# Other row pitches, offsets and product orders for the split activations of a two-layer decoder

## The chip, the cores and the metric

The kernel runs on one core of a Trainium2 chip. The metric is the device time of one execution in microseconds. Three runs of the kernel before took 2369.81 to 2370.03 us, median 2370.01 us. A core has a matrix engine (PE, with its weight loads shown as PEld), a vector engine (DVE), an activation engine (ACT), a general engine (POOL) and a queue engine (SP), which run on their own and wait for one another by semaphores. SBUF is the on-chip memory with 128 partitions; PE reads both operands from it and writes to PSUM.

## The reference

A decoder trunk of two layers over 272 tokens (16 learned meta tokens, then 256) of width 2048, 16 heads of 128. Layer 0 uses forgetting attention, layer 1 stick-breaking attention over a K/V computed once; each is followed by a squared-ReLU MLP of hidden width 8192.

```python
def squared_relu_mlp(h, w_up, w_down):
    u = h @ w_up
    return jnp.square(jax.nn.relu(u)) @ w_down

for layer in range(DEPTH):                                   # 2
    a = rms_norm(h, norm_attn[layer])
    if layer < N_A_LAYERS:                                   # layer 0
        q, k, v, f_logit = jnp.split(a @ fox_w_in[i], [D_MODEL, 2 * D_MODEL, 3 * D_MODEL], axis=-1)
        logf = jax.nn.log_sigmoid(f_logit + fox_b_f[i])
        o = forgetting_attention(q, k, v, cumsum(logf))      # softmax(q k / sqrt(128) + F_q - F_k), causal
        h = h + o @ fox_w_o[i]
    else:                                                    # layer 1
        shared_k, shared_v = jnp.split(rms_norm(h, kv_norm) @ w_kv, 2, axis=-1)
        o = stick_breaking_attention(a @ sb_w_q[i], shared_k, shared_v)
        h = h + o @ sb_w_o[i]
    h = h + squared_relu_mlp(rms_norm(h, norm_mlp[layer]), w_up[layer], w_down[layer])
return rms_norm(h, final_norm)[:, N_META:]
```

All of it is float32, and the result has to keep float32 accuracy.

## The kernel before

The residual stream lies feature major in SBUF: `hT` [128, 16 chunks, 272 tokens]. PE has a fast format, float32r, that keeps fewer bits than float32. Each float32 operand of a large product is therefore split into a high part (the value rounded to float32r) and a low part (the rest), and a product becomes three: high weights x high activations, high weights x low activations, low weights x high activations.

`new_split` (line 99) gives the split activations of one stage as a tile [128, 16 chunks, 2, 272] float32r out of a pool of two buffers: for each chunk 272 high values, then 272 low ones. A chunk row is 2 x 272 x 4 = 2,176 bytes, 8.5 times 256. In the built program the two buffers begin at bytes 92,800 and 127,616 of each partition, both 128 past a multiple of 256. Stages of layer 1 that need only the 256 real tokens skip the first 16 columns (64 bytes) of each part.

`gemm_group` (line 146) makes four output chunks of 128 features, over all of K. It goes over four quarters of K: a DMA on SP brings 512 x 512 weights (`raw`, 1 MiB), ACT rounds them to `whi` (line 174), DVE subtracts to get `wlo` (line 175), in two halves of two chunks each. For each (chunk, output) place it issues the three products of lines 195 to 197 into one of four PSUM accumulators:

```python
nc.tensor.matmul(accs[m][:, :n], wh, hi[:, k, t0:], start=first, stop=False)     # L195
nc.tensor.matmul(accs[m][:, :n], wh, lo[:, k, t0:], start=False, stop=False)     # L196
nc.tensor.matmul(accs[m][:, :n], wl, hi[:, k, t0:], start=False, stop=last)      # L197
```

With `pairs` (stages o1 and down projections of layer 1) the first two become one product of 2 x 256 columns (line 193); the evacuation then adds two halves. A stage of four groups is 4 x 64 places, so 768 products, or 512 with `pairs`.

The stages in order, with the names of their activations: q, k, v of layer 0 (`x_a`, 12 groups, attention between them), output projection (`x_o`), four blocks of up (`x_m`) and down projection (`x_u`); for layer 1 the queries (`x_a`, 256 columns), k and v (`x_kv`, 8 groups, attention between them), output projection (`x_o`, pairs), four blocks of up (`x_m`) and down (`x_u`, pairs). Layer 0 and k, v use 272 columns, the others 256.

The order on each engine is not that of the source: a scheduler that simulates the time places the instructions. Where `wlo` comes late, it puts off the products of line 197 and takes hi and lo products of further outputs first. `split_chunk` (line 103), `put_split` (line 290) and the evacuation in `mlp` (line 420) write the split activations; `Norm.finish` (line 127) makes the inverse root of the mean squares.

Of the kernel before, what the change touches and what calls it, by code (L numbers as in the profile page):

```python
# [24 lines left out]
N_FF = 4             # blocks of D columns in the hidden width  # L25
# rows of the gains
# [4 lines left out]
def yoco_kernel(ctx: ExitStack, tc: tile.TileContext, hT_in, gains, b_f, w_f, w_qkv0, w_o0, w_up, w_dn,  # L31
# [5 lines left out]
    wspl = ctx.enter_context(tc.tile_pool(name="wspl", bufs=3))  # L37
    xs = ctx.enter_context(tc.tile_pool(name="xs", bufs=2))
# [21 lines left out]
    # ntri[k', k] = -1 where k' >= k  # L60
# [6 lines left out]
    # causal mask of the first layer, on negated scores [query, key]: keys of the queries 16..143,  # L67
    # then of the queries 144..271
# [6 lines left out]
    # the same for the meta tokens of four heads, [head and query, (head, key)] with room for 32 keys  # L75
# [6 lines left out]
    # strict mask of the second layer [key, query]: keys 0..127 x queries 16..271, then  # L82
    # keys 128..255 x queries 128..271
# [6 lines left out]
    # tokens 256..271 of four heads, [head and key, (head, query)]  # L90
# [12 lines left out]
    def split_chunk(sp, gi, c, t0):  # L103
        """gain * residual chunk, as two float32r parts that add up to it"""
        hi, lo, _ = sp
        g = g_sb[:, gi, c:c + 1]
        nc.scalar.activation(hi[:, c, t0:], hT[:, c, t0:], AF.Copy, scale=g)
        nc.vector.scalar_tensor_tensor(out=lo[:, c, t0:], in0=hT[:, c, t0:], scalar=g,
                                       in1=hi[:, c, t0:].bitcast(F32), op0=ALU.mult, op1=ALU.subtract)

    class Norm:
        """sum of squares of the residual stream, chunk by chunk, and its inverse root"""
# [14 lines left out]
        def finish(self):  # L127
# [3 lines left out]
            a = tmp.tile([P, T], F32, tag="rs_a", bufs=1, name=f"rs_a_{self.label}")  # L131
            y = tmp.tile([P, T], F32, tag="rs_y", bufs=1, name=f"rs_y_{self.label}")
            t = tmp.tile([P, T], F32, tag="rs_t", bufs=1, name=f"rs_t_{self.label}")
# [12 lines left out]
    def gemm_group(wblk, sp, t0, evac, before={}, after={}, load_x=None, pairs=False):  # L146
# [4 lines left out]
        hi, lo, both = sp  # L151
# [4 lines left out]
        for kb in range(4):  # L156
# [28 lines left out]
            for kc, m in order:  # L185
                whi, wlo = parts[kc // 2]
                k = 4 * kb + kc
                wh = whi[:, kc % 2, m * P:(m + 1) * P]
                wl = wlo[:, kc % 2, m * P:(m + 1) * P]
                first = kb == 0 and kc == 0  # L190
                last = kb == 3 and kc == 3
                if pairs:
                    nc.tensor.matmul(accs[m], wh, both[:, k, :, t0:], start=first, stop=False)  # L193
                else:
                    nc.tensor.matmul(accs[m][:, :n], wh, hi[:, k, t0:], start=first, stop=False)  # L195
                    nc.tensor.matmul(accs[m][:, :n], wh, lo[:, k, t0:], start=False, stop=False)  # L196
                nc.tensor.matmul(accs[m][:, :n], wl, hi[:, k, t0:], start=False, stop=last)  # L197
                if last:
                    evac(m, [accs[m][:, :n]] + ([accs[m][:, n:]] if pairs else []))
# [5 lines left out]
    def total(acc, to):  # L205
        """the sum of the parts of a product, in SBUF if there are two"""
# [6 lines left out]
    # ================= layer 0: forgetting attention =================  # L213
    norm = Norm("a0", 0)
    xa = new_split("a0")
    box = {}

    def load_x(chunks):
        c0, n = chunks[0], len(chunks)
        nc.sync.dma_start(hT[:, c0:c0 + n, :], hT_in[:, c0:c0 + n, :])  # L220
        for c in chunks:
            split_chunk(xa, G_A0, c, 0)
# [11 lines left out]
    def forget_gates(rstd):  # L234
        """log sigmoid, running sum over the tokens"""
# [8 lines left out]
        for k in range(NC):  # L244
            nc.tensor.matmul(pf[:NC, :T], wf_hi[:, k, :], xa[0][:, k, :], start=k == 0, stop=False)
            nc.tensor.matmul(pf[:NC, :T], wf_hi[:, k, :], xa[1][:, k, :], start=False, stop=False)
            nc.tensor.matmul(pf[:NC, :T], wf_lo[:, k, :], xa[0][:, k, :], start=False, stop=k == NC - 1)
# [11 lines left out]
        # tokens 16..143 and 144..271 on the partitions  # L259
# [4 lines left out]
        # by way of DRAM for the copies to all partitions  # L264
# [4 lines left out]
    def token_major(vT, pr, t0, label):  # L269
        """tokens t0 .. t0+127 and t0+128 .. t0+255 of two heads"""  # L270
# [8 lines left out]
    def packed(src, label):  # L279
        """[128, 4, n] in consecutive columns"""  # L280
# [5 lines left out]
    def put_split(sp, h, nh, t, n, src):  # L286
        nc.scalar.activation(sp[0][:, h:h + nh, t:t + n], src, AF.Copy)
# [356 lines left out]
```

## Time and profile before

| | |
|---|---|
| median of three runs | 2370.01 us |
| span of the profiled execution | 2368.6 us |
| PE busy | 2351.3 us (99%), 17,758 matmuls |
| weight loads | 2281.5 us (96%), 17,758 |
| DVE busy | 1320.9 us (56%) |
| ACT busy | 1037.9 us (44%) |
| POOL busy | 35.1 us (1%) |
| DMA | 412 MB, 174 GB/s |

The profile tells busy time of each engine, its groups of instructions by line, the chain of work that ended last, and a timeline with the start of each instruction. Matmuls are pipelined: each lasts longer in the record than the distance to the next one's start, so the rate of PE is read from start to start. Lines (L195) are those of the kernel. An entry `acc<-x_u,whi 128*128 128x272` is a product of 128 x 128 high weights with 272 columns of `x_u` into an accumulator.

### The profile page before, as it was taken

Reading aid. Unit: us, or ns where it says so; the run is one execution under the profiler, and the core shown is the slowest. Engines: PE = TensorE matmul, PEld = TensorE weight load, DVE = VectorE, ACT = ScalarE, POOL = GpSimd, SP = SyncE. Lnnn points to the kernel's source line nnn. Section 1 sums busy time; section 2 is a strip of 40 time slices with the busy share of each in tenths; the row PEclk is TensorE's granted clock in tenths of the full one; section 3 lists DMA queues with packets and bytes.
Section 4 is the critical chain, followed back from the end, with each engine's and each line's share of the span. In section 5 each row is a group of like instructions: output and inputs, shape, how many; then the busy total and the mean of one; then the engine's idle time right before and its main releaser. Section 6 shows DMA issues by size and latency. Waiting matters only on the chain.

```text
span 2368.6 us, 41443 instructions
## 1 busy us (share of the span) xinstructions
PE 2351.3 (99%) x17758; PEld 2281.5 (96%) x17758; DVE 1320.9 (56%) x1837; ACT 1037.9 (44%) x1393; POOL 35.1 (1%) x61
## 2 busy tenths in 40 slices
PE   8999999999999999999999999999999999999998
PEld 8999999999999999999999999989989989989997
DVE  7565555655455455445565555566555555555555
ACT  5433344543344344344444444445443443543444
POOL 0000000000000000000000000000000000000000
PEclk9999999999999999999999999999999999999999
DMA  6444444554545555455555444455555555555553
GB/s 231 143 167 170 152 161 161 171 185 162 185 170 178 178 178 178 165 178 174 178 177 188 153 144 143 144 176 180 194 179 194 194 180 195 179 180 196 185 188 125
DMA packets 60872, 412.08 MB, mean 174 GB/s; under 512 B 7040, under 2 KB 9744, under 8 KB 11920
## 3 DMA queue, kind: packets, MB, share of 16 engines
q1 hardware_dynamic: 59632, 407.05, 50.3%
q8 instruction: 139, 2.28, 0.4%
q10 hardware_dynamic: 1056, 2.38, 0.3%
q14 instruction: 45, 0.37, 0.0%
HBM read 407.29 MB, written 2.11 MB: 173 GB/s over the span
## 4 chain that ended last, share of the span: by engine, by line
PE 99%; DVE 0%; DMA 0%; ACT 0%; issue 0%; SPq 0%; DVEq 0%
PE acc L197 32%; PE acc L196 25%; PE acc L195 25%; PE acc L193 12%; PE ps L332 0%; PE pza L507 0%; PE pv L274 0%; PE po L393 0%; PE po L394 0%; PE po L546 0%; DVE ob L590 0%; PE po L547 0%; PE pzb L508 0%; DMA raw<-w_qkv 0%; PE po L395 0%; PE po L548 0%
## 5 line engine op out<-in xcount | busy, mean ns | idle before, releaser
L175 DVE TENSOR_TENSOR wlo<-raw,whi 128x1024 fp32r<-128x1024 f32 (+1 forms) x770 | 934.6, 1221 | 808.7 <-ACT whi L174 806.1
L174 ACT ACTIVATE whi<-raw 128x1024 fp32r<-128x1024 f32 (+1 forms) x770 | 807.2, 1056 | 1144.1 <-PE acc L196 874.4
L196 PE MATMUL acc<-x_m,whi 128*128 128x272 f32 (+1 forms) x2048 | 577.5, 285 | 0.0
L195 PE MATMUL acc<-x_m,whi 128*128 128x272 f32 (+1 forms) x2048 | 574.6, 284 | 0.0
L197 PE MATMUL acc<-x_m,wlo 128*128 128x272 f32 (+1 forms) x2048 | 559.4, 285 | 0.0
L197 PE MATMUL acc<-x_u,wlo 128*128 128x272 f32 (+1 forms) x2048 | 537.1, 285 | 0.0
L197 PEld LDWEIGHTS acc<-x_u,wlo 128*128 128x128 f32 x2048 | 381.1, 188 | 13.5
L196 PEld LDWEIGHTS acc<-x_m,whi 128*128 128x128 f32 x2048 | 386.7, 189 | 0.0
L195 PEld LDWEIGHTS acc<-x_m,whi 128*128 128x128 f32 x2048 | 386.3, 189 | 0.3
L197 PEld LDWEIGHTS acc<-x_m,wlo 128*128 128x128 f32 x2048 | 376.2, 188 | 0.0
L193 PE MATMUL acc<-x_u,whi 128*128 128x512 f32 x1024 | 342.8, 395 | 0.0
L195 PE MATMUL acc<-x_a,whi 128*128 128x272 f32 (+1 forms) x1024 | 293.4, 290 | 6.3 <-ACT whi L174 6.3
L196 PE MATMUL acc<-x_a,whi 128*128 128x272 f32 (+1 forms) x1024 | 294.1, 291 | 0.0
L195 PE MATMUL acc<-x_u,whi 128*128 128x272 f32 x1024 | 292.6, 288 | 0.0
L196 PE MATMUL acc<-x_u,whi 128*128 128x272 f32 x1024 | 292.1, 288 | 0.0
L197 PE MATMUL acc<-x_a,wlo 128*128 128x272 f32 (+1 forms) x1024 | 284.1, 289 | 0.0
L193 PEld LDWEIGHTS acc<-x_u,whi 128*128 128x128 f32 x1024 | 186.2, 188 | 30.9
L195 PEld LDWEIGHTS acc<-x_a,whi 128*128 128x128 f32 x1024 | 193.9, 190 | 7.2 <-ACT whi L174 6.3
L196 PEld LDWEIGHTS acc<-x_a,whi 128*128 128x128 f32 x1024 | 194.2, 190 | 0.5
L196 PEld LDWEIGHTS acc<-x_u,whi 128*128 128x128 f32 x1024 | 194.0, 189 | 0.0
L195 PEld LDWEIGHTS acc<-x_u,whi 128*128 128x128 f32 x1024 | 192.7, 188 | 0.0
L197 PEld LDWEIGHTS acc<-x_a,wlo 128*128 128x128 f32 x1024 | 189.3, 189 | 0.6
(224 smaller groups left out, 2306.3 us busy)
## 6 DMA issues: line engine op xcount, KB each, us to landing
raw<-w_up SPq DMA_DIRECT2D x128, 1024.0 KB, 4.9
raw<-w_dn SPq DMA_DIRECT2D x128, 1024.0 KB, 4.9
raw<-w_qkv SPq DMA_DIRECT2D x45, 1024.0 KB, 4.9
raw<-w_o SPq DMA_DIRECT2D x32, 1024.0 KB, 4.8
raw<-w_kv SPq DMA_DIRECT2D x32, 1024.0 KB, 4.9
raw<-w_q SPq DMA_DIRECT2D x16, 1024.0 KB, 4.9
fk<-f_dram ACTq DMA_DIRECT2D x4, 544.0 KB, 5.4
raw<-w_qkv SPq DMA_DIRECT2D x4, 512.0 KB, 6.6
```

The source lines that it names most:

```text
L174: on_act = nc.scalar.activation(hp, src, AF.Copy)
L175: on_dve = nc.vector.tensor_tensor(out=lp, in0=src, in1=hp.bitcast(F32), op=ALU.subtract)
L193: nc.tensor.matmul(accs[m], wh, both[:, k, :, t0:], start=first, stop=False)
L195: nc.tensor.matmul(accs[m][:, :n], wh, hi[:, k, t0:], start=first, stop=False)
L196: nc.tensor.matmul(accs[m][:, :n], wh, lo[:, k, t0:], start=False, stop=False)
L197: nc.tensor.matmul(accs[m][:, :n], wl, hi[:, k, t0:], start=False, stop=last)
```

## The change

A class `Split` takes the place of `new_split`. Its tile has rows of 576 values (2,304 bytes, nine times 256) unless a stage asks for another pitch, and every stage names where hi and lo begin in the row, and the pitch. A new tile `pad` of 128 bytes moves both buffers to multiples of 256 (92,928 and 129,792). `PASSES` gives three orders of the three products; the up projections use order f % 3 in block f, all others order 0. Block 3 of layer 1's up projection now uses `pairs`. The start of hi and lo within 256 bytes ("residue") follows:

| stage | columns | residues of hi, lo | order |
|---|---|---|---|
| x_a, layer 0 | 272 | 64, 192 | 0 |
| x_o, layer 0 | 272 | 0, 128 | 0 |
| x_m, layer 0, f = 0..3 | 272 | 0, 64 | 0, 1, 2, 0 |
| x_u, layer 0, f = 0..3 | 272 | 0, 64 / 64, 128 / 128, 192 / 192, 0 | 0 |
| x_a, layer 1 | 256 | 0, 0 (pitch 512) | 0 |
| x_kv | 272 | 0, 64 and 128, 192 in turn (pitch 544) | 0 |
| x_o, layer 1 | pairs | 0, 64 | |
| x_m, layer 1, f = 0..2 | 256 | 0, 0 (pitch 512) | 0, 1, 2 |
| x_m, layer 1, f = 3 | pairs | 0, 0 (pitch 512) | |
| x_u, layer 1, f = 0..3 | pairs | 0, 0 / 0, 64 / 64, 64 and 192, 192 in turn / 128, 128 | |

Where lo begins 256 values behind hi, both are one run of 512 values. Besides, two temporaries of `Norm.finish` share the slots of `sq`, and the four tiles of the final norm are one. Comments are gone. The rest only passes positions through.

```diff
+XROW = 576
+
+LAYOUTS = (((0, 272), (16, 288), (32, 304), (304, 0)),
+           ((0, 256, 512), (0, 272), (16, 272, 544), (32, 288, 576)))
+
+PASSES = (lambda wh, wl, hi, lo: ((wh, hi), (wh, lo), (wl, hi)),
+          lambda wh, wl, hi, lo: ((wh, lo), (wh, hi), (wl, hi)),
+          lambda wh, wl, hi, lo: ((wh, hi), (wl, hi), (wh, lo)))
...
+    align = ctx.enter_context(tc.tile_pool(name="align", bufs=1))
     xs = ctx.enter_context(tc.tile_pool(name="xs", bufs=2))
...
-    def new_split(label):
-        t = xs.tile([P, NC, 2, T], F32R, tag="x", name=f"x_{label}")
-        return t[:, :, 0, :], t[:, :, 1, :], t
...
+    pad = align.tile([P, 32], F32, name="pad")
+    nc.gpsimd.memset(pad, 0.0)
...
+    class Split:
...
+        def __init__(self, label, t0, hi, lo, pitch=XROW):
+            self.n, self.t0 = T - t0, t0
+            t = xs.tile([P, NC * XROW], F32R, tag="x", name=f"x_{label}")
+            rows = t[:, :NC * pitch].rearrange("p (c q) -> p c q", c=NC)
+            self.hi, self.lo = rows[:, :, hi:hi + self.n], rows[:, :, lo:lo + self.n]
+            d = lo - hi
+            self.both = rows[:, :, hi:hi + 2 * d].rearrange("p c (h t) -> p c h t", h=2)[:, :, :, :self.n] \
+                if d > 0 and hi + 2 * d <= pitch else None
...
-            a = tmp.tile([P, T], F32, tag="rs_a", bufs=1, name=f"rs_a_{self.label}")
+            a = tmp.tile([P, T], F32, tag="sq", name=f"rs_a_{self.label}")
...
+                hi, lo = sp.hi[:, k], sp.lo[:, k]
                 if pairs:
-                    nc.tensor.matmul(accs[m], wh, both[:, k, :, t0:], start=first, stop=False)
+                    nc.tensor.matmul(accs[m], wh, sp.both[:, k], start=first, stop=False)
+                    nc.tensor.matmul(accs[m][:, :n], wl, hi, start=False, stop=last)
                 else:
-                    nc.tensor.matmul(accs[m][:, :n], wh, hi[:, k, t0:], start=first, stop=False)
-                    nc.tensor.matmul(accs[m][:, :n], wh, lo[:, k, t0:], start=False, stop=False)
-                nc.tensor.matmul(accs[m][:, :n], wl, hi[:, k, t0:], start=False, stop=last)
+                    for i, (w, x) in enumerate(PASSES[passes](wh, wl, hi, lo)):
+                        nc.tensor.matmul(accs[m][:, :n], w, x, start=first and i == 0, stop=last and i == 2)
...
-    xa = new_split("a0")
+    xa = Split("a0", 0, 16, 304)
...
-    ao = new_split("o0")
+    ao = Split("o0", 0, 0, 288)
...
-        xm = new_split(label)
+        xm = Split(label, t0, *((0, 272) if t0 == 0 else (0, 256, 512)))
...
-            u = new_split(f"u{layer}_{f}")
+            u = Split(f"u{layer}_{f}", t0, *LAYOUTS[layer][f])
...
-                gemm_group(w_up[layer, f, g], xm, t0, evac, {3: get_rstd} if f == g == 0 else {})
+                gemm_group(w_up[layer, f, g], xm, t0, evac, {3: get_rstd} if f == g == 0 else {},
+                           pairs=t0 == M and f == 3, passes=f % 3)
...
-            box["xq"] = new_split("a1")
-        split_chunk(box["xq"], G_A1, c, M)
+            box["xq"] = Split("a1", M, 0, 256, 512)
+        split_chunk(box["xq"], G_A1, c)
...
-    xc = new_split("kv")
+    xc = Split("kv", 0, 0, 272, 544)
...
-    ao = new_split("o1")
+    ao = Split("o1", M, 0, 272)
```

More of the change, by code (lines that the diff above doesn't have):

```diff
@@ L144, in yoco_kernel, with gemm_group @@
     uid = [0]
-    def gemm_group(wblk, sp, t0, evac, before={}, after={}, load_x=None, pairs=False):
-        hi, lo, both = sp
+    def gemm_group(wblk, sp, t0, evac, before={}, after={}, load_x=None, pairs=False, passes=0):
         uid[0] += 1
@@ L576, in yoco_kernel @@
     mlp(1, xm, norm_m, M, last_evac)
-    a, y, t, rs = (tmp.tile([P, 2], F32, tag=f"fin_{i}", bufs=1, name=f"fin_{i}") for i in range(4))
+    fin = tmp.tile([P, 4, 2], F32, tag="fin", bufs=1, name="fin")
+    a, y, t, rs = (fin[:, i, :] for i in range(4))
     nc.vector.tensor_scalar(a, pms[:, :2], EPS, None, op0=ALU.add)
```

37 lines of the change are left out of this document (18 added, 19 removed).

## The prediction

> **What bounds the kernel now.** I read the page first (shares, clock, chain), then the timeline of TensorE (PE) at the borders of the GEMM stages, then single stretches inside them. From the page:
>
> ```profile
> span 2368.6 us, 41443 instructions
> PE 2351.3 (99%) x17758; PEld 2281.5 (96%) x17758; DVE 1320.9 (56%) x1837; ACT 1037.9 (44%) x1393; POOL 35.1 (1%) x61
> PEclk9999999999999999999999999999999999999999
> PE 99%; DVE 0%; DMA 0%; ACT 0%; issue 0%; SPq 0%; DVEq 0%
> PE acc L197 32%; PE acc L196 25%; PE acc L195 25%; PE acc L193 12%; PE ps L332 0%; PE pza L507 0%; PE pv L274 0%; PE po L393 0%; PE po L394 0%; PE po L546 0%; DVE ob L590 0%; PE po L547 0%; PE pzb L508 0%; DMA raw<-w_qkv 0%; PE po L395 0%; PE po L548 0%
> ```
>
> PE is busy throughout at full clock, and 94% of the chain (32 + 25 + 25 + 12) is the GEMM products of lines 193 to 197. Busy time is pipelined, so the rate comes from start to start. The timeline of PE (start, duration, engine, line, what) at the borders of four stages:
>
> ```profile
> 540.92 0.29 PE L195 MATMUL acc<-x_u,whi 128*128 128x272 f32 x1
> ...
> 637.16 0.29 PE L195 MATMUL acc<-x_m,whi 128*128 128x272 f32 x1
> ...
> 1722.18 0.39 PE L193 MATMUL acc<-x_u,whi 128*128 128x512 f32 x1
> ...
> 1811.78 0.28 PE L195 MATMUL acc<-x_m,whi 128*128 128x256 f32 x1
> ...
> 1902.82 0.39 PE L193 MATMUL acc<-x_u,whi 128*128 128x512 f32 x1
> ```
>
> A stage is 4 groups x 64 (chunk, output) places. The first, with three 272-column products a place, takes 96.24 us: 125.31 ns per product. The third, three 256-column products, takes 91.04 us: 118.54 ns. The second, paired (a 512 and a 256 column product), takes 89.60 us: 350.0 ns a place, hence 231.5 for the 512. Windows of the first two stages:
>
> ```profile
> 541.00:637.00 96.00, 96.00 (x768) 96.00 (x767) 46.25 (x50) 34.55 (x37) 0.00 (x0) 1.00 0.52 176
> 1723.00:1811.00 88.00, 88.00 (x505) 76.98 (x504) 48.20 (x61) 32.92 (x34) 0.00 (x0) 1.00 0.56 192
> ```
>
> PE never stops; DVE (46 of 96 us) and ACT (35) have room; the clock is 1.00. So only the price of one product counts, and that is what the change touches.
>
> **Why a product costs that.** An fp32 product (two passes) of the attention, on the same timeline:
>
> ```profile
> 104.54 0.59 PE L393 MATMUL po<-pm_sb,vz 128*128 128x256 f32 x2
> 104.97 0.59 PE L394 MATMUL po<-pp_sb,v_sb 128*128 128x256 f32 x2
> ```
>
> Two passes of 256 columns take 0.43 us, 215 ns a pass. If a float32r product streams twice as fast, 256 columns would need 108 ns and 272 need 114; they take 118.5 and 125.3. About 10.5 ns of each is unexplained, and the change tries to touch it by address.
>
> Does the address matter now? In the kernel before, rows are 2,176 bytes and the built program places both x buffers 128 bytes past a multiple of 256, so the places of hi and lo within 256 bytes ("residues") alternate from chunk to chunk: 128/192, then 0/64 in layer 0; 192/0, then 64/128 where the 16 meta tokens are skipped. The timeline shows the alternation:
>
> ```profile
> 541.05 0.29 PE L196 MATMUL acc<-x_u,whi 128*128 128x272 f32 x1
> 541.17 0.29 PE L197 MATMUL acc<-x_u,wlo 128*128 128x272 f32 x1
> 541.30 0.28 PE L195 MATMUL acc<-x_u,whi 128*128 128x272 f32 x1
> ...
> 541.67 0.29 PE L195 MATMUL acc<-x_u,whi 128*128 128x272 f32 x1
> ```
>
> The first chunk (128/192, from 540.92) takes 0.38 us, the second (0/64) 0.37; over all such places the means are 378.7 and 372.9 ns. Part of that difference is only where a start is marked, because the two add up to the stage's rate. Better evidence are stretches in which the scheduler repeats hi and lo of one chunk for the four outputs (wlo was late), so that residues do not alternate. First and last of 53 such stretches with 272 columns, and of 20 with 256, each from the first start to the ninth:
>
> ```profile
> 15.15 0.29 PE L195 MATMUL acc<-x_a,whi 128*128 128x272 f32 x1
> ...
> 16.15 0.29 PE L197 MATMUL acc<-x_a,wlo 128*128 128x272 f32 x1
> ...
> 1508.74 0.29 PE L195 MATMUL acc<-x_kv,whi 128*128 128x272 f32 x1
> ...
> 1509.74 0.29 PE L197 MATMUL acc<-x_kv,wlo 128*128 128x272 f32 x1
> ```
>
> ```profile
> 1216.73 0.28 PE L195 MATMUL acc<-x_a,whi 128*128 128x256 f32 x1
> ...
> 1217.66 0.28 PE L197 MATMUL acc<-x_a,wlo 128*128 128x256 f32 x1
> ...
> 2243.49 0.28 PE L195 MATMUL acc<-x_m,whi 128*128 128x256 f32 x1
> ...
> 2244.44 0.28 PE L197 MATMUL acc<-x_m,wlo 128*128 128x256 f32 x1
> ```
>
> Their means over eight products are 124.89 ns (0.42 under the stage's rate) and 118.31 ns (0.23 under). One stretch repeats the whole triple at residue 0/64/0:
>
> ```profile
> 13.65 0.29 PE L195 MATMUL acc<-x_a,whi 128*128 128x272 f32 x1
> ...
> 13.90 0.29 PE L197 MATMUL acc<-x_a,wlo 128*128 128x272 f32 x1
> 14.03 0.28 PE L195 MATMUL acc<-x_a,whi 128*128 128x272 f32 x1
> ...
> 15.03 0.29 PE L197 MATMUL acc<-x_a,wlo 128*128 128x272 f32 x1
> ```
>
> Eleven products in 1.377 us: 125.2 ns, though the hand-over from hi to hi in it (13.90 to 14.03) is a dear one, 128 ns.
>
> **The change part by part.**
>
> *Constant residues* (row 2,304 bytes, or 2,048 for the streams of layer 1 at pitch 512; base moved to a multiple of 256). Layer 0: 9,216 products get constant residues (x_a 2,304; x_o, four x_m and four x_u stages 768 each); the 1,536 of x_kv keep a pitch of 544 and alternate as before: nothing. Layer 1: 3,072 single products at residue 0 throughout, and 1,280 paired places, 256 of which (block f=2, pitch 544) still alternate. At the prices of the stretches: 9,216 x 0.42 = 3.9 us; 3,072 x 0.23 = 0.7 us; paired places 1,280 x (0.23 + 0.45 for the 512, the same share) = 0.9 us. I take these because they are many and free of the alternation. The bounds are the dear and the cheap triple above: -1.0 to +0.9 ns a product for 272 columns (9 us either way), and for 256 columns, where the two triples average 352.8 and 359.8 ns, -0.9 to +1.4 (with the 512 in proportion, 6 to 10 us). So -15 to +18 us about the zero of today's mean.
>
> *Order of the products.* Orders 1 and 2 are rotations of the sequence hi, lo, hi; every product loads its weights in all three (17,758 weight loads for 17,758 matmuls on the page), so I price order itself at nothing. In order 2 wlo is wanted second. The built order delays those products, as it did before; if a wlo came late all the same, PE would wait for a split on DVE. The cover is the whole idle half of DVE.
>
> *Layer 1, block 3 of the up projection becomes paired*: 91.04 - 89.60 = 1.4 us less. It adds 16 copies on ACT and 16 additions on DVE. Their nearest rows:
>
> ```profile
> L203 DVE TENSOR_TENSOR hT<-acc,hT 128x256 f32<-128x256 f32 x160 | 58.4, 416 | 32.1 <-PE acc L197 31.2
> L426 ACT ACTIVATE u<-relu 128x256 f32<-128x256 f32 x64 | 26.2, 409 | 32.9 <-DVE relu L424 32.0
> ```
>
> 7 us on each, beside a stage in which each is idle half the time. An accumulator comes free some 0.8 us later; the next group first touches the last one some 24 products into its list (over 3 us), so this is hidden. Without that cover: 4 groups x 0.8 = 3.3 us.
>
> *Smaller edits.* One memset on POOL at the start (PE waits for the first weights there), two temporaries of the norms sharing other slots, four two-column tiles made one: the scheduler leaves the other engines' lists in the same order and the sum of squares is complete before its reader anyway. Nothing; uncovered, each norm would cost at most one 0.4 us step.
>
> Sum: 3.9 + 0.7 + 0.9 + 1.4 = 6.9 us less. The profiled span of 2368.6 becomes 2361.7; the median of the runs (2370.0) lies 1.4 us above the span, so 2363.1 us.
>
> **The rivals.**
>
> *Address does not matter.* Then only the pairing counts: 2370.0 - 1.4 = 2368.6 us. For it: x_u and x_m, in different buffers, cost the same 96.24 us, and in the repeated stretches single steps vary (128, 127, 125, 125, 125, 121, 123, 124) while the residues merely alternate. Against it: the stretches' means are below the stage's rate in both widths. The Trainium skill, SBUF — State Buffer, Door 1, gives 16-byte lines as the unit that an access pattern crosses; by that rule every row here, a multiple of 64 bytes before and after, is equal, and the trace neither proves nor excludes it.
>
> *Slower: the same residue twice running.* In the new kernel the last product of a place and the first of the next start at the same residue, and in layer 1 every stream starts at residue 0, so nearly every hand-over is of that kind: 3,072 in layer 0 (a third of 9,216) and 3,072 + 2 x 1,280 = 5,632 in layer 1. At 128 - 125.3 = 2.7 ns each that is 8,704 x 2.7 = 23.5 us, less the pairing 1.4: 2392 us. It shows as slower from 0.7 ns a hand-over ((4.7 + 1.4) / 8,704). Against it: the 0/64/0 stretch makes the 128 good in its other products. In layer 1 nothing makes it good.
>
> *The unexplained 10.5 ns goes.* If aligned rows stream at half the fp32 pass: 272 columns 10.8 ns less on 9,216 products (99 us), 256 columns 10.5 less on 3,072 + 1,280 (46 us), the 512 16 less on 1,280 (21 us): with the pairing some 2203 us. Against it: products at residue 0 exist now in both widths and cost no such thing. The Trainium skill, TensorE: Matmul & The Clock Gate, Wait — 56ns, not 53.3ns?, gives N/2.4 + 2.5 ns between warm matmuls, an estimate of 115.8 ns for 272 columns; the trace's 125.31 disagrees.
>
> *A larger part of the same gain* (the cheap triple everywhere): 2370 - 15 - 1.4 = 2353 us.
>
> **How the numbers follow.** Small gain by constant residues 0.38 (alone 2357 to 2368), no effect of address 0.25, slower 0.22, the larger part 0.10, the whole excess 0.05. A measurement of this kernel tells about 0.2% (4.7 us, so 2365.3 and 2374.7) from no change. Faster by more: 0.27 of the first case, and 0.15 of the last two, 0.42. Slower: 0.22. Same: the rest, 0.36. The range of 8 in 10 leaves out the whole excess and the tips of the cheap and the dear case: 2345 to 2388.
>
> **What would show it.** Stage lengths between the borders above: x_m and x_u of layer 0 near 95.9 us, x_m of layer 1 near 90.9, the last x_m stage 1.4 us shorter than its sisters. Layer 0 stages that differ from one another by over 0.3 us show that residue or order matters more than I price; layer 1 at 93 us or more shows the slower rival; stages of about 88 us in layer 0 show the whole excess gone. Gaps of PE at the starts of block 2 would show late wlo. The prediction fails if the 10 ns depend on how hi and lo stand to each other, of which the trace shows few cases.

## The result: slower by 0.17%

The changed kernel takes 2373.57 us (median of 18 runs, 2372.12 to 2374.49), the kernel before beside it 2369.59 us (2368.18 to 2370.22). The ratio is 1.0017, 95% interval 1.001 to 1.0024: 4.0 us slower, clear of noise, where 6.9 us less was forecast. The page of the changed kernel shows the same picture as before, PE busy throughout at full clock (0.998 in the mean of both):

```profile
span 2370.4 us, 40945 instructions
PE 2353.2 (99%) x17502; PEld 2269.3 (96%) x17502; DVE 1326.7 (56%) x1853; ACT 1042.5 (44%) x1409; POOL 33.5 (1%) x62
```

The time lies in the length of the stages. The timeline of PE in the changed kernel (start, duration, engine, line, what), first product of each stage of layer 0's MLP, blocks 0 to 3:

```profile
442.34 0.29 PE L218 MATMUL acc<-x_m,whi 128*128 128x272 f32 x1
...
539.28 0.29 PE L218 MATMUL acc<-x_u,whi 128*128 128x272 f32 x1
...
635.78 0.29 PE L218 MATMUL acc<-x_m,whi 128*128 128x272 f32 x1
...
732.29 0.28 PE L218 MATMUL acc<-x_u,whi 128*128 128x272 f32 x1
...
827.89 0.29 PE L218 MATMUL acc<-x_m,whi 128*128 128x272 f32 x1
...
924.84 0.29 PE L218 MATMUL acc<-x_u,whi 128*128 128x272 f32 x1
...
1021.42 0.29 PE L218 MATMUL acc<-x_m,whi 128*128 128x272 f32 x1
...
1117.92 0.29 PE L218 MATMUL acc<-x_u,whi 128*128 128x272 f32 x1
...
1213.51 0.28 PE L218 MATMUL acc<-x_a,whi 128*128 128x256 f32 x1
```

And of layer 1's MLP:

```profile
1630.32 0.28 PE L218 MATMUL acc<-x_m,whi 128*128 128x256 f32 x1
...
1721.88 0.40 PE L214 MATMUL acc<-x_u,whi 128*128 128x512 f32 x1
...
1812.12 0.28 PE L218 MATMUL acc<-x_m,whi 128*128 128x256 f32 x1
...
1904.28 0.39 PE L214 MATMUL acc<-x_u,whi 128*128 128x512 f32 x1
...
1994.29 0.28 PE L218 MATMUL acc<-x_m,whi 128*128 128x256 f32 x1
...
2085.43 0.40 PE L214 MATMUL acc<-x_u,whi 128*128 128x512 f32 x1
...
2175.54 0.40 PE L214 MATMUL acc<-x_m,whi 128*128 128x512 f32 x1
...
2266.27 0.40 PE L214 MATMUL acc<-x_u,whi 128*128 128x512 f32 x1
```

The distance from one row to the next is a stage. In the kernel before, every stage without a pause had one length for its kind (96.24 us in layer 0, 91.04 for an up block and 89.60 for a paired down block of layer 1). Now each stage has its own. The places are hi/lo within 256 bytes:

| stage (places of hi/lo) | us | against before |
|---|---|---|
| layer 0 up, blocks 1 and 3 (0/64; orders 1, 0) | 96.51, 96.50 | +0.27 |
| layer 0 up, block 2 (0/64, order 2) | 96.95 | +0.71 |
| layer 0 down, block 0 (0/64), 2 (128/192) | 96.50, 96.58 | +0.3 |
| layer 0 down, block 1 (64/128), 3 (192/0) | 95.60, 95.59 | -0.65 |
| layer 1 up, block 1 (0/0, order 1) | 92.16 | +1.1 |
| layer 1 up, block 2 (0/0, order 2) | 91.14 | +0.1 |
| layer 1 down (paired), blocks 0 to 2 | 90.24, 90.01, 90.11 | +0.4 to +0.65 |
| layer 1 up, block 3 (paired now) | 90.73 | -0.3 |

Summed over the trace (minus is less time): layer 0 without the shared k, v -1.1 us, the k, v stage nothing, layer 1 +3.9 us, the paired block -0.3, together +2.4 us. But 1.3 us of the gain in layer 0 is not the change's. In every run the first products stand about 227 ns apart before they go to about 126. Four or eight products of the first group in the kernel before, in the changed kernel, and in the changed kernel run again (e11 below):

```profile
10.06 1.11 PE L196 MATMUL acc<-x_a,whi 128*128 128x272 f32 x4
10.97 1.11 PE L197 MATMUL acc<-x_a,wlo 128*128 128x272 f32 x4
```

```profile
9.20 1.39 PE L218 MATMUL acc<-x_a,whi 128*128 128x272 f32 x8
```

```profile
9.07 2.02 PE L218 MATMUL acc<-x_a,whi 128*128 128x272 f32 x8
```

Before, four products from 10.06 us take 0.91 us. In the changed kernel the step comes sooner, so that eight products from 9.20 us take 1.39 us; in e11 eight products from 9.07 us take 2.02. The traces' records of the granted clock name full clock from 12.45, 9.67 and 11.29 us on. The first group takes 33.31 us before, 31.97 here and 32.73 in e11. Without this, layer 0 changed by +0.2 us and the whole by +3.8 us, close to the 4.0 of the medians; this is also why the profiled execution was the fastest of the 18. So the places of the activations do set a price, in steps of 0.1% to 1.2%, but not the one that I read off.

### The profile page after: what moved, and what is told of

Same layout as the page of the kernel before. It is cut to its first block, busy times and chain, and to the rows that moved or that the text cites. A ratio compares the mean times of both kernels' runs of the same rounds, so it can differ in the third digit from the quotient of the medians.

```text
span 2370.4 us, 40945 instructions
## 1 busy us (share of the span) xinstructions
PE 2353.2 (99%) x17502; PEld 2269.3 (96%) x17502; DVE 1326.7 (56%) x1853; ACT 1042.5 (44%) x1409; POOL 33.5 (1%) x62
## 4 chain that ended last, share of the span: by engine, by line
PE 99%; DVE 0%; DMA 0%; ACT 0%; issue 0%; SPq 0%; DVEq 0%
PE acc L218 72%; PE acc L214 15%; PE acc L215 8%; PE ps L353 0%; PE pza L529 0%; PE pv L295 0%; PE po L414 0%; PE po L415 0%; PE po L568 0%; DVE ob L613 0%; PE po L569 0%; PE pzb L530 0%; DMA raw<-w_qkv 0%; PE po L416 0%; PE po L570 0%; PE pf L266 0%
## 5 line engine op out<-in xcount | busy, mean ns | idle before, releaser
L218 PE MATMUL acc<-x_m,whi 128*128 128x272 f32 (+1 forms) x3584 | 654.2, 286 | 0.0
L218 PEld LDWEIGHTS acc<-x_m,whi 128*128 128x128 f32 x3584 | 553.4, 189 | 0.2
L218 PE MATMUL acc<-x_a,whi 128*128 128x272 f32 (+1 forms) x2048 | 384.6, 289 | 6.3 <-ACT whi L194 6.3
L218 PE MATMUL acc<-x_u,whi 128*128 128x272 f32 x2048 | 378.8, 288 | 0.0
L218 PE MATMUL acc<-x_u,wlo 128*128 128x272 f32 x1024 | 283.4, 287 | 0.0
L215 PE MATMUL acc<-x_u,wlo 128*128 128x256 f32 x1024 | 252.7, 281 | 0.0
L218 PE MATMUL acc<-x_kv,whi 128*128 128x272 f32 x1024 | 191.9, 289 | 0.0
L218 PEld LDWEIGHTS acc<-x_kv,whi 128*128 128x128 f32 x1024 | 159.5, 189 | 0.3
L218 PE MATMUL acc<-x_kv,wlo 128*128 128x272 f32 x512 | 144.3, 291 | 0.0
L224 DVE TENSOR_TENSOR hT<-acc,hT 128x256 f32<-128x256 f32 (+1 forms) x240 | 93.7, 425 | 69.4 <-PE acc L218 36.1
```

What stands on the lines that cost most here:

```text
L215: nc.tensor.matmul(accs[m][:, :n], wl, hi, start=False, stop=last)
L218: nc.tensor.matmul(accs[m][:, :n], w, x, start=first and i == 0, stop=last and i == 2)
L224: nc.vector.tensor_tensor(out=hT[:, c, t0:], in0=a, in1=hT[:, c, t0:], op=ALU.add)
```

## The experiments

**The old layout with the new orders and the paired block (e1_orders_pairs).** Edit, on the kernel before:

```diff
...
+    h, l = hi[:, k, t0:], lo[:, k, t0:]
+    order3 = (((wh, h), (wh, l), (wl, h)), ((wh, l), (wh, h), (wl, h)), ((wh, h), (wl, h), (wh, l)))[passes]
...
-    gemm_group(w_up[layer, f, g], xm, t0, evac, ...)
+    gemm_group(w_up[layer, f, g], xm, t0, evac, ..., pairs=t0 == M and f == 3, passes=f % 3)
```

> The old tile (row 2,176 bytes, base 128 past a multiple of 256) with the orders f % 3 of the up projections and the paired block alone. Theory 'orders have a price of their own': the up stages of block 2 in layer 0 go from 96.24 to about 96.9 us and of block 1 in layer 1 from 91.05 to about 92.2 us, as in the changed kernel. Rival 'orders cost only where all rows of a stream lie alike': both stay within 0.1 us of 96.24 and 91.05. In both cases the paired block takes 90.0 to 90.7 us in place of 91.05. Total: about 2370.5 us by the first, 2369 us by the second.

Measured 2369.35 us, ratio 0.9999 (0.999 to 1.0009). Blocks 1 and 2 of layer 0 took 96.40 and 96.42 us (+0.17), of layer 1 90.92 and 90.95 (-0.1), the paired block 90.30. So the orders and the pairing alone do not make the kernel slower, and on the alternating rows the large prices that block 2 of layer 0 (0.7 us) and block 1 of layer 1 (1.1 us) had in the changed kernel are absent. That leaves the places, which e13 below tests by themselves.

**The buffers 64 bytes further (e3_base64).** Edit, on the kernel before:

```diff
+    align = ctx.enter_context(tc.tile_pool(name="align", bufs=1))
     xs = ctx.enter_context(tc.tile_pool(name="xs", bufs=2))
...
+    pad = align.tile([P, 16], F32, name="pad")
...
```

> The kernel before with its two activation buffers moved by 64 bytes and nothing else, so that hi begins at 192 and 0+64 past multiples of 256 in layer 0 (lo at 0 and 128), and at 0 and 128 in layer 1 (lo at 64 and 192). Theory 'the place of hi within 128 bytes sets the price, 64 is cheap and 0 is dear': the stages of layer 0 fall from 96.24 to 95.2-95.6 us (the changed kernel's cheap stages: 95.6), which is 9 to 14 us over 56 groups, and the stages of layer 1 rise by up to 1%, 0 to 8 us; total 2356 to 2369 us. Rival 'only the hand-over between rows with the same place counts': every stage keeps its length within 0.1 us, total 2369.6 us.

Measured 2378.12 us, ratio 1.0037 (1.0024 to 1.005). Every full stage of layer 0 took 97.28 us (126.67 ns a product), layer 1 fell a little (90.85 and 89.32 us). My first theory after the result, hi at 64 is cheap and alternation cheaper still, is wrong: alternating 192/0 and 64/128 is dearer than any stage of the changed kernel, though each of the two alone is cheap there (95.6 us). The rival fell too, since 64 bytes moved the length of every stage by more than 0.1 us.

**The weights 64 bytes further (e4_weights64).** Edit, on the changed kernel:

```diff
+    alignw = ctx.enter_context(tc.tile_pool(name="alignw", bufs=1))
     wspl = ctx.enter_context(tc.tile_pool(name="wspl", bufs=3))
...
-    pad = align.tile([P, 32], F32, name="pad")
+    padw = alignw.tile([P, 16], F32, name="padw")
...
+    pad = align.tile([P, 16], F32, name="pad")
```

> The changed kernel with the split weights moved by 64 bytes and the activations where they were. Theory 'the price hangs on the distance between the activations' and the weights' places': the prices change places, the down stages of blocks 1 and 3 in layer 0 go from 95.60 to about 96.5 us, those of blocks 0 and 2 and the up stages from 96.5 to about 95.6 us. Rival 'the place of the activations alone': every stage within 0.1 us of the changed kernel.

Measured 2363.79 us in one run. The timeline of this kernel at the down stages of layer 0, blocks 0 to 2:

```profile
539.20 0.29 PE L221 MATMUL acc<-x_u,whi 128*128 128x272 f32 x1
...
634.78 0.29 PE L221 MATMUL acc<-x_m,whi 128*128 128x272 f32 x1
...
730.35 0.29 PE L221 MATMUL acc<-x_u,whi 128*128 128x272 f32 x1
...
826.85 0.29 PE L221 MATMUL acc<-x_m,whi 128*128 128x272 f32 x1
...
922.42 0.29 PE L221 MATMUL acc<-x_u,whi 128*128 128x272 f32 x1
...
1018.02 0.29 PE L221 MATMUL acc<-x_m,whi 128*128 128x272 f32 x1
```

95.58, 96.50 and 95.60 us where the changed kernel has 96.50, 95.60 and 96.58, and the up block between them (634.78 to 730.35) 95.57 for 96.51. Block 3 went from 95.59 to 96.58 us. The prices changed places though no activation moved. So what counts is how the activations stand to the weights, and not their own place; e10 tests this at a third place of the weights.

**Other pairs of places (e5_scan).** Edit: other numbers for the stages, and no pairing in layer 1's MLP.

```diff
+LAYOUTS = (((0, 304), (288, 0), (304, 32), (0, 272, 544, 16)),
+           ((16, 272), (16, 320), (0, 272), (0, 288)))
...
+        xm = Split(label, t0, 16, 288)
```

> Other places for hi and lo, one pair a stage, no pairing in the MLPs of layer 1. Theory 'hi at 64 past a multiple of 128 is cheap, at 0 dear; lo at the other place than hi is cheaper by 0.3-0.5 ns a product; the hand-over to the same place within 256 bytes costs 0.35 ns a product': layer 0, down blocks 0 to 3 with hi/lo 0/192, 128/0, 192/128 and alternating 64/128, 192/0: 96.5, 96.9, 95.6 and 95.3 us; up (64/128) 95.6 us for order 0; output projection (192/64) 95.8 us of products. Layer 1, down blocks with 64/64, 64/0, 0/64, 0/128: cheap, cheap, dear, dear around 91.1 us. Rival 'each pair has a price without a rule': no such pattern in the untried pairs.

Measured 2369.44 us in one run. Layer 0: 0/192 96.67 us, 128/0 95.57, 192/128 96.15, alternating 64/128 and 192/0 96.05 (e3 had the same two the other way round: 97.28); up (64/128) 95.60 and 95.67. My rule for the untried pairs held for the first and failed for the other three. Layer 1 brought the surprise: 64/64 took

```profile
1716.74 0.29 PE L218 MATMUL acc<-x_u,whi 128*128 128x256 f32 x1
...
1803.80 0.28 PE L218 MATMUL acc<-x_m,whi 128*128 128x256 f32 x1
```

87.06 us, 113.35 ns a product against 118.54 before, while 64/0, 0/64 and 0/128 took 91.2, 92.7 and 92.6 (the last stage of the layer, with some 0.9 us of waits at its end).

**Hi and lo at one place (e6_equal).** Edit: `LAYOUTS` with 64/64, 128/128, 0/0, 192/192 in layer 0 (row pitch 640, chunk k in row k % 14), and 0/0, 192/192, 64/64, 128/128 in layer 1.

> Hi and lo at the same place within 256 bytes, one place a stage, no pairing. (In the down projections of layer 0 the rows of chunks 14 and 15 are laid over those of 0 and 1, since the wider rows do not fit: that part of the result is wrong, the work is the same.) Weights at 128. Theory 'every stream 64 bytes behind the weights that are loaded beside it loses nothing': layer 0, down blocks 0 to 3 at 64, 128, 0, 192: about 92.5 us (17/16 of a column per clock, 120.4 ns a product) at 64, over 95 us at the others; layer 1: down block 2 at 64 with rows of 2,048 bytes 87.06 us, the others (queries and block 1 at 192, up projections and block 3 at 128, block 0 at 0 with rows of 2,304 bytes) over 90 us. Rival 'the row pitch of nine times 256 does it': block 0 of layer 1 falls to 87 us and block 2 stays at about 91 us.

Measured 2385.37 us in one run. This kernel lays rows of the down blocks of layer 0 over one another, so it leaves out part of their sums, and products wait at the start of each of these blocks. Down block 2 of layer 1, at 64/64 with rows of 2,048 bytes:

```profile
2098.18 0.29 PE L220 MATMUL acc<-x_u,whi 128*128 128x256 f32 x1
...
2185.24 0.28 PE L220 MATMUL acc<-x_m,whi 128*128 128x256 f32 x1
```

It took 87.06 us; the others 91.14 us at 0, 90.46 at 192, 93.04 at 128 in the last block (with the waits at its end) and 92.14 to 92.16 at 128 in the up blocks without a pause. So it is the place, not the pitch. With 272 columns the theory failed: in the groups without waits the products took 123.3 ns at 64, not 120.4; 125.3 to 126.7 at the others.

**The low weights 64 bytes further (e7_wlo64).** Edit: `wlo` out of a pool of its own behind 64 bytes of padding.

> The low weights 64 bytes further (at 192) than the high ones (at 128). Theory 'a stream's distance to the weights of the next product counts': hi at 64 and lo at 128 are then both 64 behind, because lo is followed by low weights: layer 0, down block 0 and the up projections fall from 95.6 to about 92.5 us; layer 1, down block 1 and the up projections fall to about 87.1 us, down block 0 (64/64) rises from 87.06 to over 90 us. Rival 'the distance to its own product's weights counts' or 'only hi to lo counts': down block 0 of layer 0 stays at 95.6 us, or down block 0 of layer 1 stays at 87.06 us.

Measured 2375.51 us in one run. The half that 64/64 rises was right (90.68 us for 87.06), the half that 64/128 becomes the fast one was wrong: 96.27 us in the down block, up to 97.37 in the up blocks, 90.99 in layer 1. So the rule "distance to the weights of the next product" is not enough: at 64/64 the fast price was lost when the low weights moved away from the high ones. That is no general rule either, for block 3 (192/0) fell to 94.94 us, the shortest stage of 272 columns until then.

**A version from the scans (e8_locked).** Edit, on the changed kernel:

```diff
+LAYOUTS = (((16, 288), (16, 288), (16, 288), (16, 288)),
+           ((16, 272), (16, 272), (16, 272), (16, 272)))
...
+        xm = Split(label, t0, *((16, 288) if t0 == 0 else (16, 272)))
...
-                gemm_group(w_dn[layer, f, g], u, t0, evac, pairs=t0 == M)
+                gemm_group(w_dn[layer, f, g], u, t0, evac)
```

> A version from the scans, with the right result: hi/lo at 64/128 in layer 0, 64/64 without pairing in layer 1, order 0. Theory 'a stage's price hangs on its own places alone': layer 0 124.46 ns a product (9,216 x 0.85 = 7.8 us less), layer 1 113.35 ns (3,840 single products x 5.20 = 20.0 us; 1,280 paired places of 350.0 become 340.05: 12.7 us), together 40.5 us less than the kernel before: 2329 us. Rival 'the price comes from the course of the whole run or from the neighbours of a stage': the new stages stay near 118.5 ns, total over 2355 us.

Measured 2332.22 us, ratio 0.9842 (0.9825 to 0.9858). All but one stage came as expected; two stages of layer 1, queries and a down block, with the same places:

```profile
1206.66 0.28 PE L218 MATMUL acc<-x_a,whi 128*128 128x256 f32 x1
...
1297.57 0.29 PE L218 MATMUL acc<-x_kv,whi 128*128 128x272 f32 x1
...
1707.55 0.28 PE L218 MATMUL acc<-x_u,whi 128*128 128x256 f32 x1
...
1794.59 0.28 PE L218 MATMUL acc<-x_m,whi 128*128 128x256 f32 x1
```

The queries take 90.91 us (117.78 ns a product), the down block 87.04 (113.33). The same places have two steady courses, that is, two prices of which a stage keeps one product after product; each of these two stages has one course throughout. The queries' 3.9 us too many are more than the 3.2 us by which the expectation was missed.

**A quarter of the weight columns (e9_narrow).** Edit, on the changed kernel, for the down projections of layer 0 and the up projections of layer 1 (`nw` 32):

```diff
+    nc.tensor.matmul(accs[m][:nw if kb in (1, 2) else P, :n], w[:, :nw if kb in (1, 2) else P], x, ...)
```

> The changed kernel, but in the second and third quarter of K the products load and use only 32 of the 128 weight columns, in the down projections of layer 0 and the up projections of layer 1 (a wrong result there; the activations stream as before). Theory 'the loss is the clash of a stream with the load of the next weights': those quarters lose most of it and no longer differ by place: 272 columns 120.5 to 122 ns in all four down blocks (now 125.66, 124.48, 125.75, 124.46), 256 columns 113.5 to 115 ns. Rival 'the loss is between one stream and the next': the same differences between the four blocks as now.

The timeline, first product of the second quarter and first of the fourth, 96 products apart, in down blocks 0 and 1 of layer 0 and up block 1 of layer 1:

```profile
570.24 0.28 PE L218 MATMUL acc<-x_u,whi 128*32 128x272 f32 x1
...
582.18 0.29 PE L218 MATMUL acc<-x_u,whi 128*128 128x272 f32 x1
...
762.63 0.29 PE L218 MATMUL acc<-x_u,whi 128*32 128x272 f32 x1
...
774.58 0.29 PE L218 MATMUL acc<-x_u,whi 128*128 128x272 f32 x1
...
1838.82 0.28 PE L218 MATMUL acc<-x_m,whi 128*32 128x256 f32 x1
...
1849.71 0.28 PE L218 MATMUL acc<-x_m,whi 128*128 128x256 f32 x1
```

124.4, 124.5 and 113.4 ns a product. Over all groups the four down blocks have 124.45, 124.42, 124.49, 124.44 (with full weights 125.55, 124.51, 125.75, 124.44). The three up blocks, all at 0/0, have 113.50 in every group without a wait (118.67, 120.0, 118.66). The kernel, which in these stages leaves out three quarters of the weight columns for half of K, took 2366.76 us in one run. With 32 columns the price of the four places differs by 0.07 ns in place of 1.3, as the theory said. It does not show the clash with the weight load by itself, because a product of 32 weight columns also writes a quarter of the accumulator; that the weights' place alone moves the price (e4, e10) is what speaks for the load. The sizes were right for 256 columns; for 272 124.4 stays, not 120.5 to 122, and e7 and e15 go below that with full weights (123.6). So for 272 columns the clash is not the whole story.

**The weights at 64 (e10_weights_at_64).** Edit, on the changed kernel: `bf_sb` and `fqm_sb` (64 bytes) move from the constants to the pool behind the weights.

> The changed kernel with the split weights at 64 past a multiple of 256 in place of 128 (two small constants lie elsewhere); activations, orders and pairing as in the changed kernel. Theory 'only the distance between activations and weights counts': each stage takes the price that its distance had in another run: layer 0 up (0/64) 95.6 us in place of 96.5, down blocks 0 to 3 95.6, 96.5, 95.6, 96.5; layer 1 queries and up blocks 0 to 2 (0/0, now 64 behind the weights) 87.1 us (113.35 ns a product) in place of 91.2 to 92.2; paired stages within 1 us of the changed kernel. Together about 23 us less than the changed kernel: 2350 us. Rival 'place 64 of the activations is the good one, whatever the weights': the stages of layer 1 stay over 90 us, total over 2365 us.

Measured 2353.02 us, ratio 0.9931 (0.9914 to 0.9947); expected 2350. With its activations where they were, the changed kernel is 20.6 us faster because the weights moved. Layer 0 came as forecast stage by stage. Down blocks 1 and 2:

```profile
728.73 0.29 PE L219 MATMUL acc<-x_u,whi 128*128 128x272 f32 x1
...
825.30 0.29 PE L219 MATMUL acc<-x_m,whi 128*128 128x272 f32 x1
...
921.04 0.29 PE L219 MATMUL acc<-x_u,whi 128*128 128x272 f32 x1
...
1016.63 0.29 PE L219 MATMUL acc<-x_m,whi 128*128 128x272 f32 x1
```

The down blocks of layer 0 in three runs, in us, by the places of hi and lo less that of the weights (in bytes, modulo 256):

| hi, lo less weights | weights at 128 (changed kernel) | at 192 (e4) | at 64 (e10) |
|---|---|---|---|
| 128, 192 | 96.50 (block 0) | 96.50 (block 1) | 96.51 (block 3) |
| 192, 0 | 95.60 (block 1) | 95.60 (block 2) | 95.60 (block 0) |
| 0, 64 | 96.58 (block 2) | 96.58 (block 3) | 96.58 (block 1) |
| 64, 128 | 95.59 (block 3) | 95.58 (block 0) | 95.59 (block 2) |

Each distance has one price to 0.02 us, whatever the block and the place. In layer 1 up block 2,

```profile
1980.17 0.28 PE L219 MATMUL acc<-x_m,whi 128*128 128x256 f32 x1
...
2067.22 0.39 PE L215 MATMUL acc<-x_u,whi 128*128 128x512 f32 x1
```

took 87.05 us; but block 1 90.45 (117.78 ns throughout), and the queries and block 0 changed from one course to the other at a pause in their first group (88.17 and 90.53 us).

**Once more (e11_again).**

> The changed kernel once more, to see what differs from one execution to the next. Theory 'stage prices are fixed by the places': every GEMM stage within 0.05 us of the first profile; what differs by 1 or 2 us in the total lies outside them. Rival 'prices differ from run to run': differences of 0.3 us and more in stages.

2373.57 us, span 2371.8. Every stage behind q, k, v has its length to 0.02 us again, but the last (90.42 for 90.35); q, k, v took 334.39 us for 333.63, all of it in the first group (32.73 us for 31.97), whose products stay 227 ns apart for longer at the start. So the prices of the stages are the program's, the same in both executions.

**Other low weights (e12_lows).** Edit: the `wlo` tile 256 bytes longer, and each stage names where in it the low weights begin.

> As the locked version (layer 1 at 64/64), and in layer 0 other places for hi, lo and the low weights, high weights at 128: q, k, v and the shared k, v with hi 192, lo 0, low weights 192; up blocks hi 192, lo 0, low weights 0, 64, 192, 192 (the last in order 1); down blocks 0 to 2 hi 128, lo 0, low weights 0, 64, 192, block 3 hi 64, lo 128, low weights 0; output projection hi 64, lo 128, low weights 64. Theory 'for 272 columns 192/0 with low weights at 192 is the best seen, 123.62 ns a product': those stages 94.94 us, the k, v stages together 5 us less than in the locked version; the others between 94.9 and 97.4 us; total 2322 to 2332 us. Rival 'that price belongs to the down projection alone': q, k, v stay at 124.5 ns or more, total 2330 us or more.

Measured 2329.86 us, ratio 0.9832 (0.9818 to 0.9847). 192/0 with low weights at 192 gave 123.62 ns in the up block and 123.6 in those groups of k, v and of q, k, v that the attention does not interrupt; so that price does not belong to one projection. The others lay between 124.5 and 125.5.

**The places alone (e13_places_alone).** Edit, on the changed kernel: `passes=0` and no paired block.

> The changed kernel with order 0 everywhere and without the paired block: the places alone. Theory 'a stage has more than one steady course at the same places, and where one order follows another the border can throw it into another': all up blocks of layer 0 at 96.5 us, up blocks 1 to 3 of layer 1 at one length, 91.14 us (or all at 92.16), total 2372 to 2373 us, so nearly all of the 4 us of the change. Rival 'the orders cost by themselves': the same for layer 0, and in layer 1 91.14 us for certain, total 2372.5 us. What it settles for both: the share of the places in the change's 4 us (places alone near +3 us, not near 0).

Measured 2373.63 us, ratio 1.0017 (1.0007 to 1.0026). The places alone make the whole 4 us, within the noise. (The small edits of the norms are still in this run; where the norm is finished, in the first up group of layer 0, two products stand 0.38 and 0.33 us apart from the next in the kernel before and in the changed one alike.) Block 3 of layer 1's up projection, unpaired:

```profile
2175.61 0.28 PE L218 MATMUL acc<-x_m,whi 128*128 128x256 f32 x1
...
2267.77 0.40 PE L214 MATMUL acc<-x_u,whi 128*128 128x512 f32 x1
```

Up blocks 1 to 3 of layer 1 took 92.16, 91.14 and 92.16 us, which neither expectation had. By the stages, the orders (+0.44 us in layer 0) and the pairing (92.16 - 90.73 = 1.43 us less) should make the changed kernel about 1 us faster than this run; with an interval of some 2 us either way the medians cannot tell that.

**One order for all blocks (e14_one_order).** Edit: `passes=1 if t0 else 2`, no paired block.

> The changed kernel with order 2 in all up blocks of layer 0, order 1 in all of layer 1, no paired block. Theory 'two steady courses, chosen at a border': in layer 1 all blocks run at one price, which may be 118.67 ns a product (91.14 us) although the order is 1; in layer 0 block 0 starts either course. Rival 'order 1 costs 1.35 ns a product at 256 columns and order 2 0.57 ns at 272': all blocks of layer 1 at 92.16 us, all of layer 0 at 96.95 us.

Measured 2375.05 us in one run. Layer 1, blocks 1 and 2, both now in order 1:

```profile
1813.80 0.28 PE L218 MATMUL acc<-x_m,whi 128*128 128x256 f32 x1
...
1905.96 0.39 PE L214 MATMUL acc<-x_u,whi 128*128 128x512 f32 x1
...
1995.97 0.28 PE L218 MATMUL acc<-x_m,whi 128*128 128x256 f32 x1
...
2087.11 0.40 PE L214 MATMUL acc<-x_u,whi 128*128 128x512 f32 x1
```

92.16 and 91.14 us, the same in e13 with order 0, and block 3 92.16 in both. The 1.1 us of block 1 are therefore no price of order 1 but the dear course (120.0 ns) of 0/0, which alternates with 118.67 from block to block; that blocks share a course was wrong, too. In layer 0 order 2 has a price of its own: 126.23 ns in blocks 1 to 3, against 125.66 for orders 0 and 1.

**The best of the scans (e15_best).** Edit: layer 0 with hi 192, lo 0, low weights 192 in every stage, layer 1 as in e8.

> Layer 0 with hi 192, lo 0, low weights 192, high weights 128 in every stage, layer 1 at 64/64, not paired, low weights 128; order 2 for the queries of layer 1. Theory 'the price belongs to the places': all stages of layer 0 at 123.62 ns a product, 94.94 us, that is about 7.5 us less than the run with mixed places (2329.9): 2322 us; 3.4 us less again if the queries fall into the fast course (87.5 us in place of 90.9). Rival 'the good price of the one up block was a course found by chance': several stages of layer 0 over 95.5 us, total over 2326 us.

Measured 2321.92 us, ratio 0.9799 (0.9783 to 0.9814): 47.8 us less than the kernel before it. The full stages of layer 0,

```profile
534.54 0.28 PE L220 MATMUL acc<-x_u,whi 128*128 128x272 f32 x1
...
629.48 0.28 PE L220 MATMUL acc<-x_m,whi 128*128 128x272 f32 x1
```

take 94.94 us each, as the theory had it. The queries stayed in the slow course (90.91 us) in spite of order 2.

## Why the prediction was wrong, point by point

- *What bounds the kernel* was right: PE alone, at full clock, and only the price of one product counts. Where I compared runs, the differences lay in stage lengths, in short waits and in the slow products at the start.
- *The step that failed is "constant residues".* I took the mean of stretches in which hi and lo of one chunk repeat (0.42 and 0.23 ns cheaper) as the price of constant places. Those stretches held only high weights and two of the three streams, lasted eight products, and lay at the places 128/192 and 192/0 with the weights at 128. Held for a whole stage, the two places between which layer 0 had alternated cost more than the alternation, not less: 125.66 ns at 0/64 and 125.75 at 128/192, against 125.31 alternating and the 124.89 that I had read off. The down blocks at 64/128 and 192/0 fell by 0.8 ns, twice what I had forecast; so constancy is not what sets the price. In place of 5.5 us less (3.9 + 0.7 + 0.9), layer 0 gave 0.2 us more (1.1 less with the start, which differs from one execution to the next) and layer 1 3.9 us more. The deeper fault: I looked for a property of the rows, and left out the second reader. e4 and e10 show that the price comes from how the stream stands to the weights; e9 speaks for the load beside it as the reason. The weights began at 128 past a multiple of 256 in both kernels, so the traces of either alone could not tell a row's place from its distance to the weights.
- *A slip in that sum:* the 0.9 us counts all 1,280 paired places, though the text says that 256 of them still alternate; 1,024 give 0.7 us. It changes nothing in the outcome.
- *The bounds from the dear and the cheap triple* held: +4 us lies within -15 to +18. They were wide enough for either sign; the range of 2345 to 2388 us holds the result for that reason, not because the forecast's mechanism was right.
- *The order of products at nothing* was nearly right: at 0/64 in layer 0 order 2 costs 0.44 us a block (e14) and order 1 nothing; on the alternating rows each costs 0.17 us (e1). The gaps of late low weights that I had named for block 2 did not come there.
- *The paired block* was forecast 1.4 us cheaper; from 91.04 it came to 90.73. That it saves 1.43 us against its unpaired state in e13 is luck: both are dearer than the 89.60 and 91.04 of the forecast, by about as much. Two terms are missing. The first is late low weights. Weight loads of that stage (busy, mean ns, idle before, releaser):

```profile
L215 PEld LDWEIGHTS acc<-x_m,wlo 128*128 128x128 f32 x256 | 48.1, 188 | 5.1 <-DVE wlo L195 1.6
```

  Low weights were waited for, 1.6 us in sum; three of these waits, one a group from the second on, reach the products (some 0.7 us in the stage). In e1, at the old places, the same stage has 1.7 us of such waits and took 90.30 us, 0.7 over the 89.60 of a paired stage. The second term is the price of the new place, the other 0.4 us. I had named the half-idle DVE as the cover for a late `wlo`, but looked only at the accumulators behind the 16 copies and additions. At the wait that ends at 2207.49 us (0.39 us of idle weight loading), though, DVE had not been too busy; it had stood idle itself, behind ACT, which had waited for PE:

```profile
2205.12 2.96 ACT L194 ACTIVATE whi<-raw 128x1024 fp32r<-128x1024 f32 x3 [0.98 <-PE acc L214]
2206.21 3.50 DVE L195 TENSOR_TENSOR wlo<-raw,whi 128x1024 fp32r<-128x1024 f32 x3 [1.59 <-ACT whi L194]
```

  This rounding begins 7.1 us after the start of its group, in the paired down block before it 5.7 us. Why it comes so much later was not followed further.
- *The rivals.* "Address does not matter" fell with e3 and e4. "The same place twice running" gave the right sign with the wrong cause: in e8 all streams of layer 1 share one place and most of its stages run at 113.33 ns, the fastest of all. "The unexplained 10.5 ns goes" was half right: 5.2 ns of it go at 256 columns, once the distance fits; beginning at a multiple of 256 bytes does not do it, since 0/0 is fast with the weights at 64 (e10) and slow with the weights at 128. "A larger part of the same gain" did not come either: the cheap triple lay at 0/64 (124.3 ns a product), and whole stages at 0/64 took 125.66.
- The signs named at the end worked: stages of layer 0 in one order differed by 0.9 us, which I had given as the sign that place matters more than I priced it.

## What to carry to other kernels

Where TensorE is the bound and products are short, read its price from start to start and compare it with the best stage of the same shape. For the float32r products here 2% of the kernel (2369.7 to 2321.9 us) lay in where the streamed operand stands against the weights within 256 bytes. Aligning rows to a round number was no remedy by itself; one run that gives each stage its own places told more than a rule, and each candidate is to be tried with the weights' place as the second variable. Before two profiles are compared, the slow products at the start are to be taken out: here they hid 1.3 us of 4. A stretch in which a schedule happens to repeat is thin evidence for a steady state: here the same places had two.

## What the runs showed of the hardware

The Trainium skill, TensorE: Matmul & The Clock Gate, Step-by-step: what each phase is for, says that the port for weight loads is independent, so that loading the next weights takes nothing from the running product. The runs here disagree: with 128 weight columns the price at 256 columns is 113.3 to 120.7 ns by the places (e8, e5), with 32 columns it is 113.5 where it was 118.7 and 120.0 (e9), and moving the weights alone swaps the prices of layer 0 (e4, e10).

Streams of 256 columns with hi and lo 64 bytes short of the weights' place run at 113.33 ns or at 117.78 (e5, e6, e8, e10); at 64 beyond it 117.78 was seen (e4, e6), at 128 off 118.67 and 120.0 (changed kernel, e6), at the same place 120.0 (e6). Which of two courses a stage takes is not set by its places alone, and a pause can change it: in e10 the queries went from 117.78 to 113.33 ns at the pause in their first group, and up block 0 from 113.33 to 117.78. What phase of the two readers this is, and how to force the fast course, is open: the queries of layer 1 stayed slow in e8, e12 and e15. For 272 columns the lowest prices seen are 123.3 ns (64/64, e6) and 123.61 (e15), and 124.4 with short weight loads; why they lie 10 ns over the 256-column course for 16 columns more was not found.
